# A decoder step on one core: identity transposes in TensorE's wait ahead of the shared keys and values, and another recorded order of the attention's blocks

## Chip, cores, metric

The kernel runs on one core of a Trainium2 chip. The metric is the device time of one execution in microseconds (us); less is better. TensorE is called PE here as in the profile, VectorE DVE, ScalarE ACT, GpSimd POOL, SyncE SP.

## The reference

One inference step of a two-layer decoder for 512 prompt tokens and 8 x 8 sample tokens, model width 1024, 16 heads of 64 over 4 key/value heads, window 128:

```python
def rms_norm(x, g):
    return x * rsqrt(mean(x * x, -1) + EPS) * g

def trunk(x, c, p0, ...):
    # layer 0
    h = modulate(rms_norm(x, norm_g[0, 0]), sh1, sc1)
    x = x + g1 * recurrent_block(h, ...)
    h = modulate(rms_norm(x, norm_g[0, 1]), sh2, sc2)
    x = x + g2 * swiglu(h, ffn_w_in[0], ffn_w_out[0])
    # keys and values, shared
    hk = modulate(rms_norm(x, kv_norm_g), kv_shift, kv_scale)
    k_new, v_new = rope_and_split(hk @ w_kv)
    k_all, v_all = concat(k_prev, k_new), concat(v_prev, v_new)
    # layer 1
    h = modulate(rms_norm(x, norm_g[1, 0]), sh1, sc1)
    q = rope(h @ attn_w_q)
    x = x + g1 * (sliding_sink_attention(q, k_all, v_all, sinks, p0) @ attn_w_o)
    h = modulate(rms_norm(x, norm_g[1, 1]), sh2, sc2)
    x = x + g2 * swiglu(h, ffn_w_in[1], ffn_w_out[1])
    return rms_norm(x, final_g)
```

The attention takes for each query the softmax over the keys of its window with one learned sink per head. The prompt has no earlier keys; each of the 8 sample sequences reads a cache of 128 keys and values.

## The kernel before, in words

The tokens are held in two halves, h = 0 and 1, called A and B in the order string: 256 prompt tokens and 32 sample tokens each, 288 columns. A linear layer is a set of "products": matmuls of a 128 x 128 weight block over 288 columns, three for each block, because weights and inputs are split in a high and a low part (`wh` is a converted weight tile, `h` an input tile, `mm` a PSUM tile). ACT casts the high part of a weight tile and DVE subtracts to get the low part, so each new weight unit costs both engines some time.

No engine is given its instructions where the code is written. A `Recorder` keeps every operation with its priority (its place in the recording) and a cost, and `schedule()` then lays out all five engines at once: at each step the engine whose candidate can start first takes it, out of at most 24 ready candidates (`LOOK`), weighing the start against the priority (`BETA` 0.75, line 43) and not running ahead more than `WIN` = 600 operations. What is recorded earlier thus tends to come earlier, no more than that. All operations are emitted by one helper, so they all carry line L489 in the profile; the tiles tell them apart.

Operations recorded under `when_idle` are fillers. `schedule()` takes one on PE only where the next real operation would start over `FILL` = 250 ns later; those left when the recording passes the point of `idle_end` are dropped. Before the change there is one such set, `keep_busy(200)` at the program's start: transposes of the identity into a PSUM tile that nobody reads.

The order of recording between the first feed-forward and the output projection is: `after_ffn0(h)` (line 1500) makes the statistics and the modulated input of keys and values for each half, then come the key/value products (`kvjobs`), then the blocks of the string `ATT` (line 53, read at line 1857). In it qN is the product of query block N (24 matmuls per half), aN the attention of chunk N (two heads, line 1650), sN one sample sequence per half (line 1730), f what ends the half, oN a block of the output projection; A or B is the half.

A chunk has two parts. The first: scores on PE (two heads side by side on row tiles 64 x 128, tiles `wh` for the keys and `sl` for the queries), mask and maximum on DVE (into `ta`, `tb`, with the maxima in `stat`), exponentials on ACT, sum and reciprocal on DVE, and the scaling, one of the two heads on ACT and the other on POOL or DVE. The second, `second()` at line 1693, is queued in `pend` and recorded when the next block comes: transposes of the probabilities on PE (`mm<-ident,ta` and `mm<-ident,tb`), copies out of PSUM into `td` by ACT and DVE, and the matmuls with the values (`ada<-td,sl`, column tiles 128 x 64). PE runs other blocks' matmuls between the steps; whether they last long enough is what the order decides. A sample block has the same steps in small (64 or 160 columns, tiles `reg`). The first exponential of the attention follows a load of ACT's function table.

A few lines of the chunk:

```python
            with rec.together():
...
                        T.matmul(sc[j][:, 256 * b : 256 * b + W], QT[h][c].f[r, b * P : (b + 1) * P], KT[0].f[r, k0 : k0 + W], start=True, stop=True)
...
                    S.activation(y, y, AF.Exp, bias=nm[:, 2 * b + j : 2 * b + j + 1], scale=0.125, accum_out=den[:, 2 * b + j : 2 * b + j + 1])
...
            V.reciprocal(rd, den)
...
            pend.append(second)
            flush(1)
```

Of the kernel before, what the change touches and what calls it, by code (L numbers as in the profile page):

```python
# [19 lines left out]
P = 128  # L20
# [29 lines left out]
WIN = 600  # L50

RNN = "x0 x1 x2 g0 g1 x3 y0 y1 x4 g2 g3 x5 y2 x6 y3 g4 g5 x7 y4 y5 g6 g7 y7 y6"
ATT = "q0A q2A a0A q1A q0B a2A q1B q3A a0B q2B q4A a1A a1B a4A a3A q3B a2B q5A q4B a3B q6A a5A q5B q7A a6A a4B s0A q6B a5B s1A s2A s3A q7B a7A s0B fA s2B a6B a7B s1B o0A s3B o1A o2A fB"
LOOK = {"PE": 24, "DVE": 24, "ACT": 24, "POOL": 24, "SP": 24}
NRAW = 4
FILL = 250
# [459 lines left out]
def trunk_kernel(ctx, tc, a):  # L516
    nc = tc.nc
    rec = Recorder(a["shadow"])
    V, S, G, T, Q = (Engine(rec, n, o) for n, o in (("DVE", nc.vector), ("ACT", nc.scalar), ("POOL", nc.gpsimd), ("PE", nc.tensor), ("SP", nc.sync)))
# [3 lines left out]
    pada = ctx.enter_context(tc.tile_pool(name="pada", bufs=(8 - NMM), space=bass.MemoryType.PSUM))  # L523

    def const(shape, name, dt=F32):
        return cp.tile(shape, dt, tag=name, name=name)
# [3 lines left out]
    def ps(pool=pmm, tag="mm"):  # L530
        cnt[0] += 1
        return rec.tile(pool, tag, NMM if tag == "mm" else (8 - NMM), RMM if tag == "mm" else 1, [P, 512], F32, f"{tag}{cnt[0]}")

    def aux():
        return ps()
# [10 lines left out]
    ident = const([P, P], "ident")  # L546
# [28 lines left out]
    @contextmanager  # L575
    def early(n):

        rec.bias -= n
        yield
        rec.bias += n  # L580
# [280 lines left out]
    def stats(h):  # L861
        st = tst[h][:, 0:3]
        pt = aux()

        ys = (acc[h], sq7[h].f) if h else (acc[h],)
        for i, y in enumerate(ys):
            for t, ts in enumerate(TOK):
                T.matmul(pt[0 : ts.stop - ts.start, t : t + 1], y[:, ts], ones, start=i + t == 0, stop=i == len(ys) - 1, skip_group_check=True)
        if h:
            sq7[h].done()  # L870
        V.tensor_scalar(st[:, 0:2], pt[:, 0:2], 1.0 / D, EPS, ALU.mult, ALU.add)
        V.tensor_scalar(st[0:32, 2:3], pt[0:32, 2:3], 1.0 / D, EPS, ALU.mult, ALU.add)
        spread(h)
# [11 lines left out]
    def modulated(h, gsc, gsh, how, cs=slice(0, KC), xn=None, known=False):  # L885

        batch, se, ne, ve, le = how.split()
        pick = {"V": V, "G": G}
        for c in range(cs.start, cs.stop):
            if (c - cs.start) % int(batch) == 0:  # L890
                modulated_samples(h, gsc, gsh, pick[se], slice(c, min(c + int(batch), cs.stop)), xn, known)
            t, u = xn[c] if xn else ta(), tb()
            n, v = t.f[:, 0:HP], u.f[:, 0:HP]
            hi, lo = [h4r(h)[:, c, i, 0:HP] for i in range(2)]
            if not known:
                pick[ne[c % len(ne)]].tensor_tensor(n, x[h][:, c, 0:HP], rstd[h][:, 0:HP], ALU.mult)
            if ve[c % len(ve)] == "S":
                S.activation(v, n, AF.Identity, bias=mp(gsh, c), scale=mp(gsc, c))
            else:
                V.tensor_scalar(v, n, mp(gsc, c), mp(gsh, c), ALU.mult, ALU.add)  # L900
            S.copy(hi, v)
            pick[le[c % len(le)]].tensor_tensor(lo, v, hi.bitcast(F32), ALU.subtract)
            if not xn or known:
                t.done()
            u.done()
        if known:
            xn[KC].done()
# [86 lines left out]
    def modulated_h(h, gsc, gsh, how, xn=None, known=False):  # L994
        H[h] = hkind[h](F32R)
        modulated(h, gsc, gsh, how, xn=xn, known=known)
# [37 lines left out]
    def convert():  # L1034
        u = units[nconv[0]]
        if u.raw is None:
            load_more()
        n = u.kc * P
        u.hi, u.lo = whs(), whs()
        with early(EW):  # L1040
            S.copy(u.hi.r[:, 0:n], u.raw.f[:, 0:n])
            V.tensor_tensor(u.lo.r[:, 0:n], u.raw.f[:, 0:n], u.hi.f[:, 0:n], ALU.subtract)
        u.raw.done()
        nconv[0] += 1
        nhi[0] += 1
# [220 lines left out]
    def ffn(l, g, after):  # L1266
# [228 lines left out]

        return emit

    XN = [None, None]

    def after_ffn0(h):  # L1500
        with early(EK):
            stats(h)
            XN[h] = [sl() for _ in range(KC + 1)]
            modulated_h(h, KVSC, KVSH, MK, XN[h])

    ffn0 = ffn(0, G2, after_ffn0)
    stages.append(jobs)
    stages.append(ffn0)
# [90 lines left out]
    def kv_done(h):  # L1599
        if h == 1:  # L1600
            convert()
            convert()
        modulated_h(h, L1 + SC1, L1 + SH1, MQ, XN[h], True)

# [251 lines left out]
    each = []  # L1856
    for w in ATT.split():
        h, n = "AB".index(w[-1]), int(w[1:-1] or 0)
# [77 lines left out]
        for t in ((4, 0, 1), (2, 3))[h]:  # L1936
            x_turn(t)

    def keep_busy(n):
        with rec.when_idle():  # L1940
            t = aux()
            for i in range(n):
                T.transpose(t[:, 0:P], ident[:], ident[:])


    keep_busy(200)
    with early(-DK):
        decay_rates()
    load_more(nload[0] - nconv[0] + 1)
# [154 lines left out]
```

## Time and profile before

| what | value |
|---|---|
| time, median of 3 runs | 1256.64 us (1256.27 to 1256.86) |
| the profiled execution's own time | 1259.39 us |
| its span, first to last instruction | 1257.6 us |
| mean granted TensorE clock | 0.995 |
| busy share PE, DVE, ACT, POOL | 99%, 71%, 52%, 38% |
| PE in the chain that ended last | 90% |

The profiled execution took 2.75 us more than the median of the runs. In the trace's own times the key/value products begin at 653.71 us, the scores of the first two chunks at 700.59, the last stretch of sample blocks lies between 758 and 788, and the output projection starts at 787.75. Times of the trace below are microseconds from the span's start. A row of the timeline gives the start, the duration up to the end of the last of its instructions, engine, line, operation, tiles and how many; in square brackets the idle time before it and who ended it. A row of the windows gives busy microseconds and instruction counts of PE, weight load, DVE, ACT and POOL, then the granted clock, the DMA share and GB/s.

### The profile page before, as it was taken

What the parts mean: (1) busy time and instruction counts of PE and PEld (TensorE: products, weight loads), DVE (VectorE), ACT (ScalarE), POOL (GpSimd) and SP (SyncE); (2) the same over time, 40 slices, a digit from 0 to 9 for tenths busy, and PEclk for the clock granted to TensorE, in tenths of its full rate; (3) what the DMA queues carried; (4) which work ended last, traced back from release to release, by engine and by line L of the source; (5) the groups of instructions that cost most, each with busy time, mean ns of one, the idle gap of its engine ahead of it and who ended that gap; (6) DMA issues with size and microseconds to landing.
All of it is one profiled execution on the core that took longest, in us unless ns stands there. A gap on an engine that the chain in (4) does not pass through costs nothing.

```text
span 1257.6 us, 25624 instructions
## 1 busy us (share of the span) xinstructions
PE 1243.6 (99%) x9674; PEld 1181.1 (94%) x9674; DVE 897.9 (71%) x2192; ACT 659.4 (52%) x1474; POOL 481.4 (38%) x671
## 2 busy tenths in 40 slices
PE   8999999999999999999999999999999999999997
PEld 7888999999998999999999987999999999999997
DVE  6989784776674676467579878558767658756856
ACT  4798963753342354145357678538425425524533
POOL 3478550133451453345125446100435336435510
PEclk9999999999999999999999999999999999999999
DMA  9966454417455645445423322232333323323222
GB/s 313 300 203 222 155 166 154 156 56 214 152 178 179 202 128 181 156 153 184 116 77 73 78 60 60 77 99 97 91 95 85 101 84 100 96 76 100 79 91 76
DMA packets 221838, 165.42 MB, mean 132 GB/s; under 512 B 23725, under 2 KB 206985, under 8 KB 221682
## 3 DMA queue, kind: packets, MB, share of 16 engines
q1 hardware_dynamic: 221266, 163.45, 42.4%
q8 instruction: 76, 1.25, 0.4%
q14 instruction: 48, 0.39, 0.1%
q0 software_dynamic: 448, 0.32, 0.1%
HBM read 160.85 MB, written 4.87 MB: 132 GB/s over the span
## 4 chain that ended last, share of the span: by engine, by line
PE 90%; DVE 4%; ACT 4%; issue 1%; DMA 0%; POOL 0%; DVEq 0%; ACTq 0%; SPq 0%; POOLq 0%
PE mm L489 86%; PE ada L489 5%; ACT ta L489 1%; DVE sl L489 1%; ACT sl L489 1%; DVE wh L489 1%; DVE ta L489 1%; ACT tb L489 0%; DVE tb L489 0%; ACT wh L489 0%; ACT L489 0%; DMA raw<-in_ffn_w_out_dram 0%; DVE h L489 0%; ACT td L489 0%; ACT h L489 0%
## 5 line engine op out<-in xcount | busy, mean ns | idle before, releaser
L489 PE MATMUL mm<-h,wh 128*128 128x288 f32 x4128 | 590.5, 297 | 1.1 <-DVE wh L489 0.9
L489 PEld LDWEIGHTS mm<-h,wh 128*128 128x128 f32 x4128 | 559.3, 188 | 12.9 <-issue 6.0
L489 PE MATMUL mm<-sl,wh 128*128 128x288 f32 x3218 | 461.1, 296 | 0.6 <-DVE wh L489 0.5
L489 PEld LDWEIGHTS mm<-sl,wh 128*128 128x128 f32 x3218 | 436.7, 188 | 7.5 <-issue 5.9
L489 ACT CAST wh<-raw 128x512 fp32r<-128x512 f32 (+3 forms) x388 | 268.8, 711 | 300.6 <-PE mm L489 188.4
L489 DVE TENSOR_TENSOR wh<-raw,wh 128x512 fp32r<-128x512 f32 (+3 forms) x388 | 352.7, 929 | 50.0 <-ACT wh L489 45.0
L489 POOL TENSOR_TENSOR raw<-raw 128x512 f32<-128x512 f32 x76 | 112.2, 1476 | 191.4 <-DVE wh L489 135.0
L489 DVE SCALAR_TENSOR_TENSOR x<-mm,mods,x 128x256 f32<-128x256 f32 x160 | 77.2, 483 | 125.9 <-PE mm L489 125.4
L489 POOL TENSOR_TENSOR x<-x,ta 128x32 f32<-128x32 f32 x120 | 42.4, 353 | 243.9 <-DVE ta L489 243.8
L489 POOL TENSOR_TENSOR raw<-raw,raw 128x512 f32<-128x512 f32 x76 | 113.0, 1486 | 4.2
L489 PE MATMUL mm<-tb,wh 128*128 128x288 f32 (+1 forms) x488 | 89.0, 297 | 1.6 <-DVE td L489 1.6
L489 POOL TENSOR_TENSOR td<-td,td 128x288 f32<-128x288 f32 x38 | 31.1, 820 | 131.3 <-ACT td L489 131.3
L489 PEld LDWEIGHTS mm<-tb,wh 128*128 128x128 f32 x488 | 72.8, 188 | 3.0 <-DVE td L489 2.0
L489 ACT ACTIVATE ta<-x 128x288 f32<-128x288 f32 (+1 forms) x56 | 24.3, 442 | 62.5 <-POOL x L489 44.0
L489 PE MATMUL mm<-ta,wh 128*128 128x288 f32 (+1 forms) x254 | 56.0, 297 | 0.0
L489 DVE TENSOR_TENSOR td<-mm,td 128x288 f32<-128x288 f32 x76 | 33.6, 452 | 25.4 <-PE mm L489 25.1
L489 PE MATMUL ada<-reg,cz 128*32 128x512 f32 (+1 forms) x408 | 47.2, 547 | 0.0
L489 PEld LDWEIGHTS mm<-ta,wh 128*128 128x128 f32 x254 | 41.7, 188 | 1.7 <-ACT sl L489 0.8
L489 ACT COPY td<-mm 128x256 f32<-128x256 f32 (+1 forms) x102 | 33.6, 354 | 13.9 <-PE mm L489 13.6
L489 DVE TENSOR_TENSOR sl<-td,sl 128x288 fp32r<-128x288 f32 x50 | 33.7, 674 | 6.0 <-ACT sl L489 5.7
L489 ACT ACTIVATE ta<-ta,stat 128x256 f32<-128x256 f32 (+2 forms) x72 | 32.5, 474 | 9.4 <-DVE stat L489 9.1
L489 DVE TENSOR_TENSOR mm<-mm,ta 128x288 f32<-128x288 f32 x38 | 17.7, 465 | 27.5 <-PE mm L489 27.5
(213 smaller groups left out, 1305.3 us busy)
## 6 DMA issues: line engine op xcount, KB each, us to landing
raw<-in_ffn_w_in_dram SPq DMA_DIRECT2D x88, 512.0 KB
reg<-in_ada_w_dram SPq DMA_DIRECT2D x72, 512.0 KB
raw<-in_ffn_w_out_dram SPq DMA_DIRECT2D x32, 384.0 KB
raw<-in_ffn_w_out_dram SPq DMA_DIRECT2D x32, 320.0 KB
raw<-in_rnn_w_in_dram SPq DMA_DIRECT2D x16, 512.0 KB
reg<-in_kv_ada_w_dram SPq DMA_DIRECT2D x14, 512.0 KB
wh<-in_ada_w_dram SPq DMA_DIRECT2D x24, 256.0 KB
raw<-in_rnn_w_out_dram SPq DMA_DIRECT2D x8, 512.0 KB
```

The costliest lines, as they stand in the source:

```text
L489: self.rec.add(eng, lambda: getattr(obj, name)(*map(real, args), **{k: real(v) for k, v in kw.items()}), cost, outs, ins, func, lat, port, ...
```

## The change

Two things. First, `keep_busy` takes the PSUM tile and the number, and `after_ffn0` records 24 more transposes of the identity as fillers ahead of the first half's statistics; those not used are dropped after the second half's. Second, the string `ATT` has another order.

```diff
-ATT = "q0A q2A a0A q1A q0B a2A q1B q3A a0B q2B q4A a1A a1B a4A a3A q3B a2B q5A q4B a3B q6A a5A q5B q7A a6A a4B s0A q6B a5B s1A s2A s3A q7B a7A s0B fA s2B a6B a7B s1B o0A s3B o1A o2A fB"
+ATT = "q0A q0B q1A q2A a0A a2A q1B q3A a0B q2B q4A a4A a1A a1B q3B a3A a2B q5A q4B a3B q6A a5A q5B q7A a6A a4B s0A a5B s1A s2A s3A q6B q7B a7A s0B s1B a6B fA a7B o0A s2B s3B o1A o2A fB"
...
+    def keep_busy(t, n):
+        with rec.when_idle():
+            for i in range(n):
+                T.transpose(t[:, 0:P], ident[:], ident[:])
+
     XN = [None, None]
 
     def after_ffn0(h):
+        if h == 0:
+            keep_busy(ps(pada, "ada"), 24)
         with early(EK):
             stats(h)
             XN[h] = [sl() for _ in range(KC + 1)]
             modulated_h(h, KVSC, KVSH, MK, XN[h])
+        if h == 1:
+            rec.idle_end()
...
-    def keep_busy(n):
-        with rec.when_idle():
-            t = aux()
-            for i in range(n):
-                T.transpose(t[:, 0:P], ident[:], ident[:])
-
-
-    keep_busy(200)
+
+    keep_busy(aux(), 200)
```

The programs that come out have 6290 rows on PE before and 6291 after: the arithmetic is the same, and of the 24 fillers 6 are placed. Three places matter.

The first is PE inside the first key/value products, just ahead of the products of the second weight tile (`mm_8553` and `mm_8578` are the PSUM tiles of the two products, `h_8501` the input, `wh_…` the weights' parts); this is the piece of the difference:

```order
 L489 MATMUL mm_8553<-h_8501,wh_8416 128x288
 L489 MATMUL mm_8553<-h_8501,wh_8398 128x288
+L489 MATMUL ada_8610<-ident 128x128 x6
 L489 MATMUL mm_8578<-h_8501,wh_8602 128x288
 L489 MATMUL mm_8578<-h_8501,wh_8475 128x288 x2
```

Six transposes of the identity stand where PE went straight on to `wh_8602`, which PE waits for in the profile.

The second is PE at the scores of the first two chunks, a0A and a2A (`wh_8684` or `wh_8691` holds the keys, the `sl` tiles the queries; `h_9033` and `h_9040` are the inputs of half B, `h_8814` and `h_8821` of half A). Before:

```order
L489 MATMUL mm_9204<-h_9033,wh_8931 128x288 x2
L489 MATMUL mm_9242<-wh_8684,sl_9126 128x128
L489 MATMUL mm_9244<-wh_8684,sl_9126 128x128
L489 MATMUL mm_9242<-wh_8684,sl_9126 128x256
L489 MATMUL mm_9244<-wh_8684,sl_9126 128x256
L489 MATMUL mm_9252<-wh_8684,sl_9197 128x128
L489 MATMUL mm_9254<-wh_8684,sl_9197 128x128
L489 MATMUL mm_9252<-wh_8684,sl_9197 128x256
L489 MATMUL mm_9254<-wh_8684,sl_9197 128x256
L489 MATMUL mm_9204<-h_9033,wh_9009 128x288
L489 MATMUL mm_9265<-h_8814,wh_9078 128x288 x2
```

After:

```order
L489 MATMUL mm_9252<-h_8821,wh_9085 128x288 x2
L489 MATMUL mm_9252<-h_8821,wh_9175 128x288
L489 MATMUL mm_9294<-wh_8691,sl_9133 128x128
L489 MATMUL mm_9296<-wh_8691,sl_9133 128x128
L489 MATMUL mm_9294<-wh_8691,sl_9133 128x256
L489 MATMUL mm_9296<-wh_8691,sl_9133 128x256
L489 MATMUL mm_9304<-wh_8691,sl_9237 128x128
L489 MATMUL mm_9306<-wh_8691,sl_9237 128x128
L489 MATMUL mm_9304<-wh_8691,sl_9237 128x256
L489 MATMUL mm_9306<-wh_8691,sl_9237 128x256
L489 MATMUL mm_9316<-h_9040,wh_9009 128x288 x2
L489 MATMUL mm_9316<-h_9040,wh_9138 128x288
```

Before, the scores stand inside q1B, with the rest of q1B (1 matmul), q3A (24) and 22 of q2B still to come, 47 in all, until the first transposes of a0A; now q3A stands ahead of the scores, and q2B follows. Further on in the program after, where the first transposes of a0A come (`mm_9316` is q2B, `mm_9374` q4A):

```order
L489 MATMUL mm_9316<-h_9040,wh_9138 128x288
L489 MATMUL mm_9374<-h_8821,wh_9167 128x288 x2
L489 MATMUL mm_9381<-ident,ta_9310 128x128
L489 MATMUL mm_9374<-h_8821,wh_9262 128x288
L489 MATMUL mm_9374<-h_8821,wh_9167 128x288
L489 MATMUL mm_9387<-ident,ta_9314 128x128
```

The first transpose of a0A's probabilities now has 24 matmuls of q2B and 2 of q4A between itself and the scores, 26 in all instead of 47.

The third is PE in the stretch of sample blocks, where the last two weight blocks of the queries are done (`ada<-td,sl` are the value matmuls of a5B, `mm<-wh,sl` the scores, 128 columns for half A and 256 for half B). Before:

```order
L489 MATMUL ada_10486<-td_10470,sl_8789 64x128 x2
L489 MATMUL ada_10486<-td_10463,sl_8997 64x128 x2
L489 MATMUL ada_10486<-td_10472,sl_8997 64x128 x2
L489 MATMUL ada_10486<-td_10477,sl_8999 64x128 x2
L489 MATMUL mm_10508<-wh_8684,sl_10130 128x128
L489 MATMUL mm_10510<-wh_8684,sl_10130 128x128
L489 MATMUL mm_10508<-wh_8684,sl_10130 128x256
L489 MATMUL mm_10510<-wh_8684,sl_10130 128x256
L489 MATMUL mm_10522<-wh_8684,sl_10322 128x256
L489 MATMUL mm_10524<-wh_8684,sl_10322 128x256
L489 MATMUL mm_10522<-wh_8684,sl_10322 128x256
L489 MATMUL mm_10524<-wh_8684,sl_10322 128x256
```

After:

```order
L489 MATMUL mm_10356<-h_9040,wh_9895 128x288
L489 MATMUL mm_10484<-ident,ta_10338 128x128
L489 MATMUL mm_10484<-ident,ta_10338 32x128
L489 MATMUL ada_10491<-td_10438,sl_8796 64x128 x2
L489 MATMUL ada_10491<-td_10436,sl_9004 64x128 x2
L489 MATMUL ada_10491<-td_10451,sl_9004 64x128 x2
L489 MATMUL ada_10491<-td_10459,sl_9006 64x128 x2
L489 MATMUL mm_10508<-wh_8691,sl_10137 128x128
L489 MATMUL mm_10510<-wh_8691,sl_10137 128x128
L489 MATMUL mm_10508<-wh_8691,sl_10137 128x256
L489 MATMUL mm_10510<-wh_8691,sl_10137 128x256
L489 MATMUL mm_10416<-td_10516,reg_9949 128x64 x2
```

Before, no product stands any nearer than 22 rows ahead of these; the scores of a7A and a6B stand side by side and the sample blocks' small matmuls come after both. After, 16 matmuls of q7B stand ahead (the last of them is the first row), the small matmuls come right behind a7A's scores, and a6B's scores stand only behind twelve rows of them.

## The prediction

> **What bounds the kernel now.** I read the head of the page first, then the waits of PE, then windows and the timeline at the places where the order changes.
>
> ```profile
> span 1257.6 us, 25624 instructions
> PE 1243.6 (99%) x9674; PEld 1181.1 (94%) x9674; DVE 897.9 (71%) x2192; ACT 659.4 (52%) x1474; POOL 481.4 (38%) x671
> PE 90%; DVE 4%; ACT 4%; issue 1%; DMA 0%; POOL 0%; DVEq 0%; ACTq 0%; SPq 0%; POOLq 0%
> ```
>
> PE is busy 99% of the span and holds 90% of the chain that ended last. No instruction of the real work on PE is taken away (6290 rows before, 6291 after), so the time can move only where PE waits, where its clock is low, or where the number of fillers adds to it. The waits of PE over the whole program are few:
>
> ```profile
> PE mm L489 <- DVE td L489: 1.7, 3, 0.9
> PE mm L489 <- DVE wh L489: 1.4, 3, 0.7
> ```
>
> Of the larger ones these two belong to the two stages touched: 0.7 us for a weight tile in the key/value products, and parts for the copies `td` of the attention. Then the clock, in windows of 100 us around it and of 4 us inside it:
>
> ```profile
> 700.00:800.00 100.00, 99.41 (x860) 86.74 (x861) 79.67 (x367) 75.72 (x273) 44.25 (x97) 0.97 0.23 64
> 800.00:900.00 100.00, 99.93 (x758) 97.79 (x755) 70.51 (x170) 56.51 (x135) 16.99 (x22) 1.00 0.27 83
> ...
> 776.00:780.00 4.00, 3.82 (x28) 2.70 (x24) 3.37 (x19) 2.72 (x13) 3.23 (x8) 1.00 0.13 38
> 780.00:784.00 4.00, 3.87 (x20) 2.12 (x20) 2.03 (x8) 2.67 (x10) 1.08 (x7) 0.60 0.68 196
> 784.00:788.00 4.00, 4.00 (x26) 2.78 (x25) 2.22 (x18) 1.34 (x6) 0.90 (x2) 0.54 0.64 191
> 788.00:792.00 4.00, 4.00 (x34) 3.99 (x34) 3.48 (x20) 3.74 (x16) 0.71 (x1) 1.00 0.28 77
> ```
>
> The third number from the right, 0.60 and 0.54 in two of the rows, is the granted clock. At half clock 0.60 stands for 0.40/0.5 x 4 = 3.2 us, 0.54 for 3.7: about 6.9 us at half clock, from 780.8 to 787.7, in the last stretch of sample blocks. What it costs is half of that, **about 3.3 us** (estimate, 3.1 to 3.4), since PE is busy there. That is the largest single loss in the attention, and the change reorders exactly this stretch.
>
> **The change part by part.**
>
> *The fillers.* The wait that they stand in:
>
> ```profile
> 653.71 3.52 PE L489 MATMUL mm<-h,wh 128*128 128x288 f32 x20
> 657.91 1.72 PE L489 MATMUL mm<-h,wh 128*128 128x288 f32 x11 [0.68 <-DVE wh L489]
> ...
> 776.89 0.61 PE L489 MATMUL mm<-ident,ta 128*128 128x128 f32 x4
> 777.45 0.44 PE L489 MATMUL mm<-ident,reg 128*128 128x128 f32 x2
> ```
>
> A transpose of this size follows the one before every 0.11 us (four take 0.61, of which one alone takes 0.27: 0.34/3). Six are 0.66 us, beside an idle time of 0.68 that ends with DVE's `wh`. DVE is not touched by them. They cost 0; if PE came so late to them that nothing of the wait were left they would cost the whole 0.66, and they cannot gain anything there by their time, since the products behind them wait for DVE as before. The clock stays 1.00 around that wait already, so holding it brings nothing. I take 0, range 0 to 0.66.
>
> *The start of the attention.* The cover of the first two chunks:
>
> ```profile
> 700.59 1.58 PE L489 MATMUL mm<-wh,sl 64*128 64x128 f32 x16
> 702.10 6.54 PE L489 MATMUL mm<-h,wh 128*128 128x288 f32 x47
> 708.48 0.27 PE L489 MATMUL mm<-ident,ta 128*128 128x128 f32 x1
> ...
> 702.55 1.28 ACT L489 ACT_TABLE_LOAD   x1 [3.87 <-DVE stat L489]
> 703.85 0.40 ACT L489 ACTIVATE ta<-ta,stat 128x128 f32<-128x128 f32 x1
> 706.49 0.49 ACT L489 ACTIVATE ta<-ta,stat 128x256 f32<-128x256 f32 x1
> 707.44 0.80 ACT L489 ACTIVATE ta<-ta,stat 128x128 f32<-128x128 f32 x2 [0.37 <-DVE stat L489]
> ```
>
> Scores start at 700.59, transposes at 708.48, 7.89 us later; between them the scores' 1.51 us and 47 products at 6.38/47 = 0.136. With 26 products (order after) PE arrives 1.51 + 26 x 0.136 = 5.05 us after the start of the scores. The probabilities are not ready then. The chain is: table load 1.96 us after the scores' start (ACT idle 3.87 before, so it started when DVE's first maxima were there), 1.28 for the load, the exponentials of a0A, then some of a2A, DVE's reciprocal, the scale on ACT from +6.85 to about +7.25. In the order after, two instead of three of a2A's exponentials stand ahead of the scale on ACT, so it can start when the third, at 706.49, would have started: +5.90, and end at +6.30; the release of PE has so far come a little behind. PE then waits 6.30 - 5.05 = 1.25 us, or up to 7.25 - 5.05 = 2.2 if the reciprocal again comes as late as in this trace, where DVE did rotary work ahead of it. I take **+1.4**, near the lower end, because fewer products are evacuated beside it. Before, PE did not wait here (ACT's scale ends 0.6 us ahead of the transposes). What was moved ahead, q3A, is not lost: those 24 products are done earlier and cost the same.
>
> *The other chunks of the attention.* In the order after, some pairs have less between them: by a count of rows, a4A's value matmuls come about 1.1 us behind its last transposes, where the copies (0.37 on ACT) and their releases take about as long. For a0A itself nothing bad is seen. I take +0.2, from 0 to +1.
>
> *The sample stretch, without the clock.* Two waits stand in it (the last product before it, some small steps and the scores behind it are shown too, for the clock):
>
> ```profile
> 769.42 0.38 PE L489 MATMUL mm<-h,wh 128*128 128x288 f32 x1
> ...
> 770.65 0.30 PE L489 MATMUL mm<-ta,reg 128*64 128x160 f32 x1
> ...
> 772.89 0.27 PE L489 MATMUL mm<-ident,reg 128*32 128x128 f32 x1
> 773.44 0.28 PE L489 MATMUL mm<-ident,reg 128*32 128x128 f32 x1 [0.28 <-ACT td L489]
> 773.65 1.09 PE L489 MATMUL ada<-td,sl 128*64 128x128 f32 x16
> 774.68 1.79 PE L489 MATMUL mm<-wh,sl 64*128 64x128 f32 x16
> 776.40 0.66 PE L489 MATMUL mm<-td,reg 128*128 128x64 f32 x4
> ...
> 778.07 0.66 PE L489 MATMUL mm<-td,wh 128*128 128x64 f32 x4 [0.18 <-DVE td L489]
> 778.56 0.61 PE L489 MATMUL mm<-td,reg 128*128 128x64 f32 x4
> 779.10 1.13 PE L489 MATMUL mm<-wh,reg 32*128 32x256 f32 x4
> 780.16 0.44 PE L489 MATMUL mm<-ident,reg 128*128 128x128 f32 x2
> ...
> 783.58 2.08 PE L489 MATMUL mm<-wh,sl 64*128 64x256 f32 x8
> ```
>
> From start to start they cost 0.55 - 0.11 = 0.44 and 778.07 - 777.45 - 0.22 = 0.40, together 0.84. In the order after, 16 products of q7B (16 x 0.136 = 2.2 us) stand behind a5B's transposes, so the first of them is covered; the second place has other small steps in its stead. I take **-0.8** for both and small gains of the same kind, with ends -1.2 and 0. The rest, from the output projection on, is the same work in the same order but for two sample blocks of half B that now run beside the output projection: 0.
>
> Sum without the clock: 0 + 1.4 + 0.2 - 0.8 = **+0.8 us**, ends 0 + 1.2 + 0 - 1.2 = 0 less what else may go well, say -1, and 0.66 + 2.2 + 1 + 0 = 3.9, of which +2.5 is as far as I go, since not all go wrong together.
>
> *The clock.* It goes down at 780.8 without a single idle microsecond: in the 4 us before it PE is busy 3.82. But what it did there was small: from the end of the scores at about 776.2 until 780.4 only matmuls of 64 to 256 columns by few rows, and transposes. [...] Before, such work lasts from 776.4 to 780.4, 4.0 us, with products last at 769.4. After, 16 products stand ahead of it, and the scores of a6B end it sooner: between a7A's scores and a6B's stand two sets of four value matmuls (776.40 to 776.89 and 778.07 to 778.56, 0.49 each), four pairs of transposes (0.22 each), s3A's four value matmuls (0.5) with the four of 256 columns (779.10 to 780.16, 1.06), and s0B's matmuls of 160 columns (0.30). Together 3.7 us, against 4.0 before. So the stretch is hardly shorter, only better surrounded: the clock can fall there still.
>
> [...]
>
> **The rivals.** *The forecast:* the clock does after what it does before, in the runs that are timed, whether it falls in both or in neither. Time +0.8 (-1 to +2.5).
>
> *The fall of the clock goes.* For it: 16 products ahead, a7A's transposes together with a6B's and a7B's scores in one piece, no chunk of transposes at the end. Against: the 3.7 us above. It gives -3.3 + 0.8 = -2.5 (-4.2 to -0.9).
>
> [...]
>
> *The change does nothing.* Only 6 of 24 fillers are placed, inside a wait, and the attention could hide all: 0. It lies within the forecast's range.
>
> **How the numbers follow.** The sum counts against the profiled execution, 1259.39 us of its own: +0.8 makes 1260.2. The median of the runs is 2.75 lower, and I carry the difference over unchanged: 1256.64 + 0.8 = **1257.4**. The second case makes 1254.1, the third 1260.7, nothing 1256.6. Chances: forecast and nothing together 0.50, the fall goes 0.32, the fall new 0.18. Within 0.2% is within 2.5 us, about what a measurement of this kernel can tell from no change. Of the second case half, 0.16, is beyond that, 0.16 inside; of the first 0.04 lies below, 0.42 inside and 0.04 above; the third is all above. Faster 0.20, I give 0.24, as the loss of two intervals may be larger than 3.3 where other engines wait too; within 0.54; slower 0.22. The range goes from 1253.6, about the middle of the lower half of the second case, to 1260.6, close to the middle of the third; about 0.2 lie outside. The forecast's own range is 1255.6 to 1259.1.
>
> **What would show it right or wrong.** Fillers: in the trace after, six transposes between the two groups of products at 653 to 660 us, and the next products start at the same distance from the first as before (4.20 us); later by over 0.3 means that they cost. Start of attention: the first transposes of a0A come 6.3 to 7.3 us behind the start of the scores with a wait of 1.2 to 2.2 put down to ACT or POOL `ta`/`tb`; without it the stretch gains 1.4. Sample stretch: no wait for ACT `td` between a5B's transposes and its value matmuls. Clock: windows of 4 us from 772 to 796 with the granted clock at 1.00 throughout mean the second case, around 0.5 for two of them the first or third. The prediction is wrong if the clock falls at another place of the program, or if copies behind the moved chunks make PE wait by more than 1 us at any place that I gave 0.

## The result, and the profile after

The changed kernel takes 1259.03 us in the median of 22 runs (1257.99 to 1261.45), the kernel before 1256.68 us beside it (1255.21 to 1259.94). The two medians lie 2.35 us apart; the ratio of the runs is 1.0014, with a 95% interval from 1.0008 to 1.0020: about 1.8 us slower, inside the 0.2% that the prediction called no change. 1257.4 was forecast, 1.6 us less than measured; the range of 1253.6 to 1260.6 holds the time.

The head of the page of after. PE is the bound as before, and the fillers raise its count by six:

```profile
span 1257.4 us, 25635 instructions
PE 1242.8 (99%) x9680; PEld 1181.1 (94%) x9680; DVE 897.3 (71%) x2192; ACT 659.0 (52%) x1474; POOL 480.0 (38%) x671
PE 90%; ACT 4%; DVE 4%; issue 1%; DMA 0%; POOL 0%; DVEq 0%; ACTq 0%; SPq 0%; POOLq 0%
```

The profiled execution of after took 1259.17 us of its own, that of before 1259.39: by the two profiles alone nothing happened. By the runs after is slower. What sets the two profiles apart from the runs is the clock. The windows of after over the sample stretch, 4 us each, with the granted clock as the third number from the right:

```profile
776.00:780.00 4.00, 4.00 (x43) 3.08 (x41) 3.83 (x18) 3.54 (x10) 3.72 (x7) 1.00 0.16 42
780.00:784.00 4.00, 4.00 (x30) 2.88 (x29) 3.46 (x15) 3.75 (x20) 3.65 (x8) 1.00 0.19 59
784.00:788.00 4.00, 3.97 (x35) 2.88 (x33) 3.48 (x23) 3.65 (x15) 0.94 (x5) 1.00 0.11 30
```

It stays at 1.00, where it was 0.60 and 0.54 in the profile of before. But the executions of before that are timed mostly lack that fall too, as the first experiment suggests; its profiled execution was one of a few.

The waits of PE over the whole program of after. There is a new group, ACT's `ta`, with 1.4 us:

```profile
PE mm L489 <- ACT ta L489: 1.4, 2, 1.1
PE mm L489 <- DVE td L489: 1.4, 2, 0.8
PE mm L489 <- DVE wh L489: 0.7, 2, 0.5
PE mm L489 <- POOL ta L489: 0.4, 1, 0.4
```

Where they stand, in the timeline of PE of after: the key/value products with the fillers, the start of the attention with both waits for ACT's `ta`, and two places of the sample stretch.

```profile
653.88 3.65 PE L489 MATMUL mm<-h,wh 128*128 128x288 f32 x21
657.37 0.82 PE L489 MATMUL ada<-ident 128*128 128x128 f32 x6
658.22 1.72 PE L489 MATMUL mm<-h,wh 128*128 128x288 f32 x11
...
704.18 1.58 PE L489 MATMUL mm<-wh,sl 64*128 64x128 f32 x16
705.69 3.72 PE L489 MATMUL mm<-h,wh 128*128 128x288 f32 x26
710.52 0.33 PE L489 MATMUL mm<-ident,ta 128*128 128x128 f32 x1 [1.10 <-ACT ta L489]
...
737.49 0.33 PE L489 MATMUL mm<-ident,ta 128*128 128x128 f32 x1 [0.32 <-ACT ta L489]
...
743.81 0.38 PE L489 MATMUL mm<-h,wh 128*128 128x288 f32 x1
...
769.82 0.44 PE L489 MATMUL mm<-ident,ta 128*128 128x128 f32 x2 [0.36 <-POOL ta L489]
...
771.67 0.35 PE L489 MATMUL mm<-ta,reg 128*64 128x160 f32 x1
771.84 0.35 PE L489 MATMUL mm<-tb,reg 128*64 128x160 f32 x1
```

The fillers fill the wait, and the products behind it start no later relative to their stage: 658.22 - 653.88 = 4.34 us behind the first product. At the start of the attention PE is idle for 1.10 us, put down to ACT's `ta`, the scaling of a0A. And the same first matmul of q6A that before started at 741.88:

```profile
741.88 0.92 PE L489 MATMUL mm<-h,wh 128*128 128x288 f32 x5
```

now starts at 743.81, 1.93 us later, of which 0.31 was there already when the key/value products began (653.88 against 653.58; 653.58 is the first product of before, and the row at 653.71 in the prediction starts with the second).

### The profile page after: what moved, and what is told of

The parts are those of the page before. It is cut to its first block, busy times and chain, and to the rows that moved or that the text cites. A ratio compares the mean times of both kernels' runs of the same rounds, so it can differ in the third digit from the quotient of the medians.

```text
span 1257.4 us, 25635 instructions
## 1 busy us (share of the span) xinstructions
PE 1242.8 (99%) x9680; PEld 1181.1 (94%) x9680; DVE 897.3 (71%) x2192; ACT 659.0 (52%) x1474; POOL 480.0 (38%) x671
## 3 DMA queue, kind: packets, MB, share of 16 engines
q8 instruction: 76, 1.25, 0.4%
## 4 chain that ended last, share of the span: by engine, by line
PE 90%; ACT 4%; DVE 4%; issue 1%; DMA 0%; POOL 0%; DVEq 0%; ACTq 0%; SPq 0%; POOLq 0%
PE mm L489 86%; PE ada L489 5%; ACT ta L489 1%; DVE ta L489 1%; ACT sl L489 1%; ACT tb L489 1%; DVE sl L489 1%; ACT L489 1%; DVE tb L489 0%; DVE wh L489 0%; DMA raw<-in_ffn_w_out_dram 0%; DVE td L489 0%; ACT td L489 0%; ACT wh L489 0%; DVE stat L489 0%
```

## The experiments

The theory, called "order" below: all of the loss comes from the new order, +1.6 us from the start of the attention, where the chain scores, maxima, table load, exponentials, scaling no longer fits behind 26 products; fillers 0. Rivals: the fillers cost (called "fillers" below); the loss lies in the sample stretch; the clock. For each kernel below the text gives the median of those executions in which the mean clock of the whole program was 0.998 or more, because an execution with a fall of the clock (0.995 or less) is a different thing to compare. The text calls this "at full clock". In the profiles of before and after the clock is at half at the program's end, behind PE's last matmul (0.50 from 1252 to 1256 us in before, 0.55 in after), where it costs PE nothing, so the mean does not reach 1.00 even without a fall. The mean tells how much of the clock was lost and not where. Before takes **1256.7 us** there (53 of 77 executions of this section), after **1258.9** (19 of 22): 2.2 us apart.

**Before again.** No edit.

> The kernel before, unchanged, so that the clock of each of its timed executions can be read. Theory A (the fall of TensorE's clock near 780 us comes only in part of its executions): two groups of times, near 1256.6 us with a mean clock of 0.997 to 0.998, and near 1259 us with 0.995; the ratio to before is 1.000. Rival B (the fall comes in each execution): the mean clock is 0.995 in all, and the spread of times has another cause.

Median 1257.65 us, 1.0008 of before (0.9999 to 1.0018). Theory A holds in the main: of the 77 executions of before in this section 53 had a clock of 0.998 or 0.999, median 1256.7; nine had 0.995 or less, median 1259.4. Fifteen had 0.996 or 0.997 and took 1256.75 to 1259.67, a group that theory A did not foresee. Where the fall lies is seen in profiles alone: near 780 us in those of before and of the fillers alone, both at 0.995. The profile of this kernel, at 0.996, is one without the fall at 780 us, in the windows from 776 on, and with a short one soon after the program's start instead:

```profile
12.00:16.00 4.00, 3.14 (x23) 2.85 (x24) 2.56 (x13) 3.70 (x7) 0.00 (x0) 0.85 1.08 345
16.00:20.00 4.00, 4.00 (x30) 3.83 (x28) 2.83 (x11) 1.04 (x2) 0.00 (x0) 0.73 1.10 352
776.00:780.00 4.00, 3.82 (x31) 2.87 (x28) 3.56 (x21) 2.61 (x12) 3.45 (x8) 1.00 0.14 40
780.00:784.00 4.00, 3.71 (x26) 2.33 (x27) 2.41 (x10) 3.04 (x12) 1.47 (x7) 1.00 0.52 157
```

The same program, row for row, with the same 3.82 us of work in the four microseconds ahead, once falls and once does not. So the work alone does not decide it; what else does is not shown. In before the fall lasts 6.8 us, from 780.8 to 787.7, at a granted clock of 0.50. What it costs is read from these two traces of one program: from the first key/value product to the last blocks of the output projection (o2B) the fall makes 2.4 us, not the 3.3 of the prediction. A part of the difference is seen: at full clock PE waits 0.29 us for DVE's `stat` at 782.34, and with the fall it does not wait there.

**Fillers only.** The first part of the diff, with the old string `ATT`.

> The old order of the attention with the 24 fillers; on PE six transposes in the key/value wait are the only difference from before. Theory 'order' (all of the +1.8 us comes from the new order): within 0.3 us of before, the products behind the wait start 4.2 to 4.35 us after the first as before. [...]

Median 1257.16 us, 1.0001 of before (0.9993 to 1.0010); 1256.4 us at full clock. The fillers cost nothing and gain nothing. Its profile has the fall (0.52 and 0.63 from 780 to 788), and two of its eleven executions had a clock of 0.995, so the fillers do not keep it away either. PE in the key/value stage of this kernel:

```profile
653.04 3.64 PE L489 MATMUL mm<-h,wh 128*128 128x288 f32 x21
656.52 0.82 PE L489 MATMUL ada<-ident 128*128 128x128 f32 x6
657.37 1.73 PE L489 MATMUL mm<-h,wh 128*128 128x288 f32 x11
```

The products behind the wait start 4.33 us behind the first; before it was 657.91 - 653.58 = 4.33.

**Order only.** The new string, no fillers.

> The new order of the attention without the fillers. Theory 'order': the same time as with both, 1.0010 to 1.0020 of before, no fall of the clock near 780 us, a wait of about 1.1 us ahead of the first transposes of a0A. Rival 'fillers': less than 1.0007 of before.

Median 1259.45 us, 1.0018 of before (1.0009 to 1.0027), all eleven executions at 0.998 or more. The whole effect is the order's.

**Start only.** The new string up to s0A, the old from there on:

```diff
-ATT = "q0A q2A a0A q1A q0B a2A ... s0A q6B a5B s1A s2A s3A q7B a7A s0B fA s2B ..."
+ATT = "q0A q0B q1A q2A a0A a2A ... s0A q6B a5B s1A s2A s3A q7B a7A s0B fA s2B ..."
```

> The new order up to s0A and the old order from there on, no fillers; the start of the attention is then the new one and the sample stretch the old one. If the start carries +1.6 us, as the shift of the PE work up to q6A in the trace has it: 1.0010 to 1.0015 of before, a wait of about 1.1 us ahead of a0A's first transposes, and a fall of the clock near 780 us in part of the executions as before. Rival (the loss lies in the sample stretch): within 0.4 us of before.

Median 1258.56 us, 1.0012 of before (1.0004 to 1.0021), 1.9 us above before at full clock. The start alone carries nearly all. Its PE row is that of after:

```profile
703.11 1.58 PE L489 MATMUL mm<-wh,sl 64*128 64x128 f32 x16
704.62 3.73 PE L489 MATMUL mm<-h,wh 128*128 128x288 f32 x26
709.45 0.33 PE L489 MATMUL mm<-ident,ta 128*128 128x128 f32 x1 [1.10 <-ACT ta L489]
```

The fall of the clock that I expected in part of its executions came in none of eleven; with nine in 77 before, that tells nothing.

**Sample stretch only, whole and in two parts.** All with the old start, without fillers. e5 has the new string from s0A on, e6 only q6B moved, e7 only what comes behind a7A:

```diff
-s0A q6B a5B s1A s2A s3A q7B a7A s0B fA s2B a6B a7B s1B o0A s3B o1A o2A fB
+s0A a5B s1A s2A s3A q6B q7B a7A s0B s1B a6B fA a7B o0A s2B s3B o1A o2A fB
...
+s0A a5B s1A s2A s3A q6B q7B a7A s0B fA s2B a6B a7B s1B o0A s3B o1A o2A fB
...
+s0A q6B a5B s1A s2A s3A q7B a7A s0B s1B a6B fA a7B o0A s2B s3B o1A o2A fB
```

> The old order up to s0A, the new one from there on, no fillers. If the sample stretch costs what the change's time lacks beside the start (after less start alone, 0.3 to 0.7 us): near 1257.1 us in the executions with a mean clock of 0.998 or more, where before takes 1256.7; and no execution at 0.996 or less, so that the spread upward is gone. Rival, the prediction's own term for this stretch (-0.8 us): near 1256.0 in those executions.

> The old order, but with q6B recorded behind s3A, directly ahead of q7B; all else as before, no fillers. If the new waits of the sample stretch (0.5 us for POOL's scaling of s0A, 0.6 us for ACT's copies of the sample keys) come from the product block that no longer stands between the steps of s0 to s3: +0.3 to +0.8 us at equal clock, and the fall of the clock goes. Rival (they come from the later part, where s1B and s2B change places): 0 at equal clock, and the fall stays in a part of the executions.

> The old order, but behind a7A the new one (s0B s1B a6B fA a7B o0A s2B s3B), no fillers. If the loss of the sample stretch lies with q6B: 0 or a gain of up to 0.4 us at equal clock. Rival: +0.3 to +0.8 us at equal clock.

e5: 1258.40 us, 1.0005 of before (0.9996 to 1.0014), 1258.4 at full clock: neither of the two figures expected, but 1.7 above before. e6: 1257.64 us, 1.0001 (0.9992 to 1.0010). e7: 1257.26 us, 0.9998 (0.9989 to 1.0006). None had an execution at 0.995 or less. The waits of PE from 758 to 812 us, first in e6 and then in e7:

```profile
PE mm L489 <- POOL ta L489: 0.9, 2, 0.6
...
PE mm L489 <- DVE stat L489: 0.3, 1, 0.3
PE mm L489 <- ACT td L489: 0.3, 1, 0.3
PE mm L489 <- DVE td L489: 0.2, 1, 0.2
PE mm L489 <- ACT ta L489: 0.2, 1, 0.2
```

The first three rows of e7 are those of before again (e1). So it is the move of q6B that takes these waits away and brings those for POOL's `ta` in their stead. What e5 loses is not in the stretch, but behind it. PE and SP's queue there, first in e5:

```profile
790.31 0.91 PE L489 MATMUL mm<-h,wh 128*128 128x288 f32 x5
792.56 0.41 PE L489 MATMUL mm<-ident,reg 128*128 128x128 f32 x2 [1.34 <-DMA reg<-in_cache_k_dram]
...
786.53 1.91 SPq L489 DMA_DIRECT2D reg<-in_cache_k_dram  x1
788.96 0.42 SPq L489 DMA_DIRECT2D reg<-in_cache_k_dram  x1
```

and the same place in after, where the transposes of the same cached keys do not wait:

```profile
792.38 0.91 PE L489 MATMUL mm<-h,wh 128*128 128x288 f32 x5
793.13 0.38 PE L489 MATMUL mm<-ident,reg 128*128 128x128 f32 x2
...
789.00 0.61 SPq L489 DMA_DIRECT2D reg<-in_cache_k_dram  x1
790.12 0.42 SPq L489 DMA_DIRECT2D reg<-in_cache_k_dram  x1
```

In e5 the keys of one of the last two sample blocks (s2B and s3B, moved behind o0A) arrive 3.6 us after their issue (788.96 to 792.56). In after PE came 3.0 us after the issue and they were there. So the new place of s2B and s3B, right behind a load whose issue took 1.9 us in the one and 0.6 in the other, lies at the edge of a wait of over a microsecond. In none of the other profiles with s2B and s3B behind o0A (after, order only, e7, table early) does PE wait for these keys. Whether the wait comes in each execution of e5 is not known beyond its times.

The times hold a second thing, outside the attention. In the profiles of order only, e5 and e6 the second feed-forward has a wait that the other seven lack, and the PE work behind it is 1.0 to 1.4 us later. First ACT and PE in order only, then ACT in after:

```profile
907.94 0.73 ACT L489 CAST wh<-raw 128x640 fp32r<-128x640 f32 x1 [2.08 <-DMA raw<-in_ffn_w_out_dram]
909.35 1.74 PE L489 MATMUL mm<-h,wh 128*128 128x288 f32 x11 [1.07 <-ACT td L489]
...
906.61 0.73 ACT L489 CAST wh<-raw 128x640 fp32r<-128x640 f32 x1 [0.60 <-PE mm L489]
```

A weight tile lands late there, ACT waits 2.08 us for it, and PE waits for ACT. How many of the timed executions have this wait is not known. So medians of eleven executions that differ by 1 us or less, as those of e6 and e7 at full clock do from before (1.0 and 0.5 above), decide nothing about the sample stretch. The marks in the traces do.

How far the PE work is shifted against the profile of before without the fall (e1), worked out from the starts of the first matmul of each block in the two traces, in us, less the shift at the first key/value product:

```
first matmul of     after  start only  e5     e6     e7     table early
a0A's transposes    +1.73  +1.77   0.00  +0.01  -0.01  +0.44
q6A                 +1.61  +1.66   0.00  +0.01  -0.02  +0.01
o0A                 +0.52  +1.63  -1.05  +0.64  -0.26  -0.99
o1B                 +1.52  +1.64  +1.47  +0.02  +0.07  +0.01
```

At q6A and at o1B all kernels have the same number of matmul rows done, 709 and 1297 from the first key/value product on, fillers not counted. At o0A after has done 1075 and before 1089, at a0A's transposes 405 and 401. Read downwards: after loses 1.61 by q6A, has won 1.1 back at o0A and has lost 1.0 of that again at o1B. The products of o0A start earlier because s2B and s3B, which stood in part ahead of them, now stand behind. When all of that is done, at o1B, the new sample stretch has neither won nor lost anything worth naming: 1.61 and 1.52. The same holds for each half of it, e6 and e7 (0.02 and 0.07 at o1B), and for e5 but for its wait for the keys.

**After, with the table loaded early.** The changed kernel with one line more behind q0A's rotary work:

```diff
             rope(h, o, [(slice(0, HC), q.f[:, 0:HC])])
+            if c == 0 and h == 0:
+                S.activation(tst[1][:, 3:4], ones, AF.Exp)
```

> The changed kernel, with one more instruction on ACT behind q0A: an exponential of one column, so that the function table is loaded some 10 us ahead of a0A's maxima. PE's order stays row for row that of after. If the wait of 1.1 us is the chain of a0A with the table load in it: the wait is gone or under 0.2 us and the time falls by 0.9 to 1.3 us against after, to about 1257.8. Rival (the wait is set by DVE's reciprocal behind other work, or by POOL): the wait stays above 0.7 us and the time within 0.4 us of after.

Median 1257.38 us, 1.0001 of before (0.9992 to 1.0010); 1257.3 at full clock, 1.6 less than after, where 0.9 to 1.3 was expected. The two were timed beside different runs of before; against those they take 1.0014 and 1.0001. `schedule()` put the load still earlier than I had meant, at 664.43 us. The start of the attention in this kernel, PE and then ACT:

```profile
703.43 1.58 PE L489 MATMUL mm<-wh,sl 64*128 64x128 f32 x16
704.94 3.73 PE L489 MATMUL mm<-h,wh 128*128 128x288 f32 x26
708.51 0.31 PE L489 MATMUL mm<-ident,ta 128*128 128x128 f32 x1
...
664.43 1.28 ACT L489 ACT_TABLE_LOAD   x1
705.41 0.40 ACT L489 ACTIVATE ta<-ta,stat 128x128 f32<-128x128 f32 x1 [11.18 <-DVE stat L489]
708.05 1.18 ACT L489 ACTIVATE ta<-ta,stat 128x128 f32<-128x128 f32 x3
```

and ACT in after, for comparison:

```profile
706.14 1.28 ACT L489 ACT_TABLE_LOAD   x1 [11.09 <-DVE stat L489]
707.44 0.40 ACT L489 ACTIVATE ta<-ta,stat 128x128 f32<-128x128 f32 x1
710.08 1.18 ACT L489 ACTIVATE ta<-ta,stat 128x128 f32<-128x128 f32 x3
```

In after the first exponential starts 3.26 us behind the scores, here 1.98: the 1.28 of the load are out of the chain. PE's order is the same row for row and its wait of 1.10 is gone. By the table above all of the shift up to q6A is gone as well (+0.01), the smaller waits behind it with it.

## Why the prediction was right, and where not

- *The bound.* Right: PE holds 90% of the chain before and after, and what moved the time were waits of PE and its clock.
- *Fillers: 0.* Right, by the fillers alone (1.0001) and by 4.33 us from the first product to those behind the wait, with and without them.
- *Start of the attention: +1.4.* Right, in the mechanism too. PE came 705.69 - 704.18 + 26 x 0.137 = 5.07 us behind the scores' start (5.05 forecast), the transposes at 6.34 (6.3 to 7.3 forecast). The difference, 1.27 us, is what the prediction called the wait (1.25 to 2.2); the profile counts 1.10 of it as idle and puts it down to ACT `ta`. That two of a2A's exponentials stand ahead of ACT's scaling set it at the lower end, as reckoned.
- *The other chunks: +0.2.* Right by sum, 1.61 us to q6A against 1.6, and not by its reason. What stands behind the first wait is a second one for ACT's `ta`, 0.32 us at 737.49, and not a4A's copies; it is gone too when the table is loaded early. Start alone shows the same 1.66 with the old sample stretch, so the place is settled, and the table load shows the cause.
- *Sample stretch: -0.8.* Wrong: 0. The step that failed is "the first of them is covered; the second place has other small steps in its stead. I take -0.8 for both". The two waits did go, but with q6B moved behind them the sample blocks' own steps have less cover: PE waits for POOL's scaling of s0A at 769.82 (0.36 idle) and comes apart at 771.67, where two pairs of matmuls that elsewhere stand 0.01 us apart start 0.17 apart. That the move of q6B brings the wait for POOL is shown by e6 and e7; why the pairs come apart is not shown. And "The rest, from the output projection on, is the same work in the same order ... 0" hid that work moved past o0A: the 1.1 us that the new stretch wins up to o0A (1.61 to 0.52) come back behind it (0.52 to 1.52). A gain read at a mark is one only if the same work stands ahead of the mark on both sides.
- *The clock.* The case of the forecast, the clock doing after what it does before, holds for most executions, which have the fall neither before nor after. But I carried the 2.75 us between the profiled execution and the median over unchanged, as if it belonged to taking a profile; most of it was the fall itself, which cost 2.4 us. Between the two profiles it is the second case that happened, at 1259.39 to 1259.17. The third case, the fall new at 1260.7, is shown by no run: of the 77 executions with the new stretch or a part of it none had a mean clock of 0.995 or less. Nor does a run show the "two intervals" beside the chances; what the trace of before shows is one fall of 6.8 us.
- *The time.* The forecast was +0.8 us; the runs show +1.8 by the ratio and 2.35 between the medians. The largest part of the difference that is known is the sample stretch's missing 0.8; a further 0.3 gathers behind o1B, where after is 1.52 us behind before without the fall, to 1.84 at the last matmul. 1259.03 lies near the upper end of the forecast's own range (1259.1), and well inside the stated range only because that was drawn wide for the two cases of the clock, which did not decide the time. That part is luck.
- *That the new stretch keeps the clock up.* Expected as possible, not shown for certain. Of the executions with the new stretch or a part of it (after, order only, e5, e6, e7 and table early, 77 in all) none had a clock of 0.995 or less, of those with the old stretch whole nine in 77 of before, two in eleven with fillers and none in eleven of start only. At 0.996 or 0.997 are six of those 77, 15 of the 77 of before and two with fillers; where their clock was low is not known but for the one profile of before again.

What is open: the fall stands in the profile of before and not in that of before again, so one cannot say from the profiles of before and after whether the program or the moment kept it away in after. The counts of executions speak for the program, none in 77 against nine in 77 of before; but start only, with the old stretch, had none in eleven either, so it is not shown. Table early is still about 0.6 us above before at full clock, with no shift left at o1B; 0.4 of it gathers from there to the last matmul, during the second feed-forward, and no experiment was made on that.

No kernel was clearly faster than before: the version with the table loaded early only returns to it, and its start of the attention is worth no more than the old one, which had the load behind 47 products anyway.

## What to carry to other kernels

When blocks are put in another order on a saturated engine, count the time between a step and its answer in work of that engine, and compare it with the longest chain of the others, once-only pieces such as a function table's load among them: 21 products less of cover cost 1.6 us here, and one dummy activation gave them back. Before a profile is compared with a median, look for what that one execution had that the others lack; the mean clock of each execution told it here. And take gains only at marks that have the same work ahead of them.

## What was not expected of the hardware

The clock of TensorE fell to 0.50 at 780.8 us in the profile of before, though the profile shows TensorE busy for 3.82 us of the 4 from 776 to 780. The same program did so in one profiled execution and not in another (before again, 1.00 from 776 to 788), and nine of its 77 timed executions had a mean clock of 0.995 or less. That fall of 6.8 us at half clock cost 2.4 us. In after the load of ACT's function table that belongs to the first exponential did not start while ACT was idle for 11.09 us ahead of it; it started at 706.14 us, when that exponential's own input, DVE's `stat`, was there.
